# Values of mixer A and of mixer B's first group: from two transposed unit products to one product by tokens, with the rows carried to their blocks by transfers

## The chip, the cores and the metric

The kernel runs on one core of one Trainium2 chip. A core has TensorE (PE, the matrix products), VectorE (DVE), ScalarE (ACT), GpSimd (POOL) and SyncE (SP), which here only issues transfers, and 16 DMA engines that carry them out. Each engine takes its instructions strictly in the order in which the program has them. The metric is the device time of one execution in microseconds (us).

## The reference

One encoder layer over 512 tokens of 1024 channels, all in float32. What matters here is its first third: every mixer multiplies probabilities by values, and the values are columns of one product `h @ w_in`.

```
proj = h @ w_in[l]
qa, ka, va, qb, kb, vb = jnp.split(proj, SPLITS, axis=-1)
...
va = va.reshape(b, s, A_KV_HEADS, HEAD_DIM)
...
vb = vb.reshape(b, s, B_NG, B_HEADS_PER_GROUP, HEAD_DIM)
o_a = windowed_gqa_sink(qa, ka, va, a_sink[l])
o_b = dilated_mixture(qb, kb, vb)
```

Mixer A has 4 value heads of 64, 256 columns, and works in blocks of 128 tokens with a window of 128 to each side. Mixer B has 3 groups of 256 value columns, with windows and strides (128,1), (512,4) and (2048,16). Then come gates, an output product, a layer norm, a SwiGLU channel mixer of 2816 columns and a second layer norm. The change touches only how `va` and the first third of `vb` come about.

## The kernel before, in words

**Precision.** Every float32 operand is split into a high and a low part (h and l), and each product is three matmuls: high by high, high by low, low by high. So a weight tile of 128x512 is loaded into a staging slot, copied to its high part (ACT, or DVE where ACT is taken) and subtracted for its low part (DVE) before TensorE can use it.

**Order of the tokens.** The 512 tokens stand in x in four runs of 128: run r holds the tokens 4i+r. A block of 128 neighbouring tokens, which mixer A and B's first group need, therefore has 32 rows from each run.

**Products by features.** `feat_x` (line 466) makes 128 features of all 512 tokens: 8 steps of 3 matmuls of 512 columns (lines 456 to 458), with the weights as the stationary operand. Queries, keys and gates are made so. Values are wanted the other way round, with tokens on the partitions. Before the change `turned_values` (line 584) made two such units, evacuated each with its columns reordered into blocks, turned every block with two transposes on TensorE (line 611) and split the turned block into h and l with `value_split` (line 624). It ran once for mixer A ("VA") and, much later, once for B's first group ("V0"). The values of B's two dilated groups already came from `token_values` ("V"): x as the stationary operand and 512 value columns moving (lines 650 to 652), which gives 128 tokens by 512 columns at once; dilated groups can use a run of tokens as it is.

**Who sets the order.** The string `ORDER` (line 74) lists the steps: `q1` is a unit of queries, `k1` of keys, `T` turns up to four units by their rotary angles (for each unit two small SBUF-to-SBUF transfers there, line 485, and two back, line 506, with work on DVE between), `G` is a unit of gates, `A0` mixer A's heads 0 to 3 in four blocks, `B0` a head of mixer B. Each step hands its operations with a priority and a guessed cost to a list scheduler (`Program.run`), which writes one order for each engine at build time. Weights are asked for early (130 us of product time ahead, constant `LOOK`), as far as 6 staging slots and 16 slots for split weights allow. All loads and all small transfers go through the one queue of SP, and at most eight of its transfers are under way: each waits for the one eight places ahead of it.

**Inside a step of mixer A** (`unit_a`): scores on TensorE (lines 578, 579), scaling and maximum on DVE (line 726), exponential on ACT (line 730), reciprocal (733) and normalising on DVE or ACT (lines 666, 668), four transposes of probabilities (678), a copy (333) and a subtraction (683) to split them, and the product with the values (743, 744).

**The first group.** Before the second product of the program, three units are made together in eight steps as x arrives: the first of keys, the first of queries and the first of VA's two (`psk, psq, psv`, line 939).

Of the kernel before, what the change touches and what calls it, by code (L numbers as in the profile page):

```python
# [13 lines left out]
ALU = mybir.AluOpType  # L14
# [44 lines left out]
SPIN = 4  # L59

CUTS = ((0, 128), (128, 256), (256, 512))
FIRST = {("k", 0): (-1000, -998.2, -997.2), ("q", 0): (-998.8, -998.1, -997.1), ("v", 0): (-998.7, -998, -997),
         ("k", 1): (-996.9,), ("q", 1): (-996.7,), ("v", 1): (-996.6,),
         "x": (-999.9, -998.5, -997.5, -996.95, -996.8, -996.5, -996.4, -996.3)}
N_WS, N_WHL, N_ATT, N_WHL1, N_TWO = 6, 16, 16, 40, 4

# [31 lines left out]
class Program:  # L98
# [16 lines left out]
    def op(self, alts, fn, reads=(), writes=(), prio=0.0, after=(), abs_prio=None, moves=0.0):  # L115
        o = Op()
        o.urgent = self.urgent
        o.alts, o.fn = alts, fn
        o.prio = (self.T + prio if abs_prio is None else abs_prio, len(self.ops))
        o.ready, o.done, o.eng = 0.0, None, None  # L120
        deps = set(a for a in after if a is not None)
        for t in reads:
            deps.update(self.writer.get(t, ()))
        for t in writes:
            deps.update(self.writer.get(t, ()))
            deps.update(self.readers.get(t, ()))
# [162 lines left out]
def hybrid_layer(ctx: ExitStack, tc: tile.TileContext, wpack, xT, xtok, sink, bgate,  # L289
# [54 lines left out]
    def cp_alts(n, ps=False):  # L344
        return [(ACT, act(n, ps)), (DVE, dve(n, not ps))]
# [74 lines left out]

    first = {}
    for j in range(2):
        for w, u in (("k", U_KA), ("q", U_QA), ("v", U_VA)):
            first[w, j] = half_unit_by(u, j, ((0, S),) if j else CUTS, FIRST[w, j])
    for j in range(KD):
        st, ap = slot(F32, "xs"), FIRST["x"][j]
        load(st, xT[j], abs_prio=ap)
        th, tl = xtok_of(j)
        op(cp_alts(S), lambda e, j=j, st=st: copy(e, xh[j](), st.t), reads=[st], writes=[th], abs_prio=ap)
        op([(DVE, dve(S))], lambda e, j=j, st=st: nc.vector.tensor_tensor(  # L430
            xl[j](), st.t, f32(xh[j]()), op=ALU.subtract), reads=[st, th], writes=[tl], abs_prio=ap)
    cosT, sinT, mA, mB = slot(), slot(), slot(), slot()
# [32 lines left out]
    def feat_x(ps, wu):  # L465
        for k in range(KD):
            feat_k(ps, wu, k, XM, xtok_of)
# [113 lines left out]
        return go, [(qt, "h"), (qt, "l"), (kt, "h"), (kt, "d"), (kl, "h"), (kl, "d")]  # L581


    def turned_values(u, nt, turn_by=0, done=None):

        src = []
        w = S // nt
        for i in range(2):
            ps = done
            if i or not done:  # L590
                ps = bank("dense")
                feat_x(ps, unit(u + i))
            t = slot()

            def evac(e, t=t, ps=ps):
                s = view(ps.t, nt, True)
                if turn_by:
                    copy(e, view(t.t[:, turn_by * w:], nt - turn_by, False), s[:, :nt - turn_by])
                    copy(e, view(t.t[:, :turn_by * w], turn_by, False), s[:, nt - turn_by:])
                else:  # L600
                    copy(e, view(t.t, nt, False), s)

            op(cp_alts(S, True), evac, reads=[ps], writes=[t], prio=EV)
            src.append(t)
        res = []
        for b in range(NR):
            pb = bank("tb")

            def turn(e, pb=pb, b=b):
                for i in range(2):  # L610
                    nc.tensor.transpose(pb.t[:, i * P:(i + 1) * P], src[i].t[:, b * P:(b + 1) * P], ident.t)

            op([(PE, 0.22)], turn, reads=[*src, ident], writes=[pb])
            res.append(value_split(pb))
        return res

    def value_split(pb, c0=0):

        t = slot(F32R)
        v = lambda: t.t.rearrange("p (h c) -> p h c", h=4)  # L620
        s = lambda: pb.t[:, c0:c0 + 256].rearrange("p (h c) -> p h c", h=4)
        op(cp_alts(256, True), lambda e: copy(e, v()[:, :, 0:64], s()), reads=[pb],
           writes=[(t, "h"), (t, "room")], prio=EV)
        op([(DVE, dve(256))], lambda e: nc.vector.tensor_tensor(
            v()[:, :, 64:128], s(), f32(v()[:, :, 0:64]), op=ALU.subtract),
           reads=[pb, (t, "h")], writes=[(t, "l")], prio=EV)
        return t

    def vtok(t):
        return [(t, "h"), (t, "l")]  # L630

    def token_values():

        parts_ = []
        for k in range(KD):
            st, h, l = slot(F32, "ws"), slot(F32R, "whl"), slot(F32R, "whl")
            u, c = U_VB + k // 4, (k % 4) * 256
            load(st, wpack[u:u + 3:2, :, c:c + 256].rearrange("g p c -> p g c"),
                 dst=lambda st=st: st.t.rearrange("p (g c) -> p g c", g=2), prio=-LOOK)
            split(st, h, l, prio=-LOOK, hold=[(l, "room")])  # L640
            parts_.append((h, l))
        res = ([], [])
        for r in range(NR):
            ps = bank("dense")
            for k in range(KD):
                wh, wl = parts_[k]

                def go(e, ps=ps, k=k, wh=wh, wl=wl, r=r):
                    a, b = xh[k]()[:, r * P:(r + 1) * P], xl[k]()[:, r * P:(r + 1) * P]
                    mm(ps.t, a, wh.t, start=(k == 0), stop=False)  # L650
                    mm(ps.t, a, wl.t, start=False, stop=False)
                    mm(ps.t, b, wh.t, start=False, stop=(k == KD - 1))

                op([(PE, 3 * pe(S))], go, reads=[wh, wl, *xtok_of(k)], writes=[ps])
                pr.T += 3 * pe(S)
            for g in range(2):
                res[g].append(value_split(ps, 256 * g))
        return res


# [275 lines left out]
        feat_x(ps, unit(u))  # L936
        return env["turn"].add(ps, *post)

    psk, psq, psv = bank("dense"), bank("dense"), bank("dense")
    for k in range(KD):  # L940
        for w, ps in (("k", psk), ("q", psq), ("v", psv)):
            feat_k(ps, [first[w, 0], first[w, 1]], k, XM, xtok_of)
    env = {"gate": 0, "qs": {}, "ks": {}, "turn": Turn()}
    ka = env["turn"].add(psk, k_post, 4)
    qa = env["turn"].add(psq, q_post, 4, (0, 0))
    load(mB, maskb, prio=0)

    def step(w):
        if w == "T":
            env["turn"].turn()  # L950
            env["turn"] = Turn()
        elif w == "VA":
            env["va"] = turned_values(U_VA, 4, 0, psv)
        elif w[0] == "q":
            i = int(w[1])
            kv = (i // 2) % 2
            qa.extend(dense(U_QA + i, q_post, 4, (kv, kv)))
        elif w == "k1":
            ka.extend(dense(U_KA + 1, k_post, 4))
        elif w[0] == "A":  # L960
            g = int(w[1])
            for b in range(NR):
                unit_a(g, b, qa[4 * g:4 * g + 4], ka[g], env["va"])
        elif w[0] in "gG":
            for _ in range(int(w[1:] or 1)):
# [634 lines left out]
```

## Time and profile before

| what | value |
|---|---|
| median of 3 runs | 781.69 us (781.56 to 782.1) |
| the profiled execution | 781.53 us, of which its span, first to last instruction, is 779.8 us |
| granted TensorE clock | 0.998 |
| TensorE | 769.9 us busy, 4486 matmuls |
| VectorE | 652.5 us busy |
| ScalarE | 480.9 us busy |
| transfers issued by SP | 429 rows of its queue |

In the profile a group of instructions stands in one row: line, engine, operation, output and input tile, shape and count, then the busy time of the group in us and the mean of one in ns, then the idle time of the engine ahead of them with what ended it. Rows of the timeline give the start in us, the length, the engine and the operation; "x8" means eight in a row. SPq is the queue of transfers on SP: its length is the time that SP needs to issue one, and its landing comes later. A matmul's length overlaps with the next one's, so its pace is read from the distance of two starts.

### The profile page before, as it was taken

The numbers are of one execution on the slowest core, as the hardware profiler recorded it, in microseconds if no ns is written. First come the engines' busy times: TensorE is split into PE (matmuls) and PEld (weight loads), VectorE is DVE, ScalarE is ACT, GpSimd is POOL, SyncE is SP. The second block draws the span as 40 slices with busy tenths as digits, with TensorE's granted clock in tenths as the row PEclk, the third lists the DMA queues.
The fourth block names the chain that finished last, engine by engine and source line by source line (L and its number), as shares of the span: only waits on it lengthen the run. The fifth ranks groups of instructions, "written<-read, shape, count | busy, mean of one in ns | idle before, by whom it ended". The sixth has DMA issues, their size and how long they took to land.

```text
span 779.8 us, 13408 instructions
## 1 busy us (share of the span) xinstructions
PE 769.9 (99%) x4486; PEld 676.6 (87%) x4486; DVE 652.5 (84%) x1377; ACT 480.9 (62%) x1061; POOL 131.5 (17%) x304
## 2 busy tenths in 40 slices
PE   9999999999999999999999999999999999999996
PEld 5888888888888888888888899999999999999985
DVE  5689889898778999797687999887988889888697
ACT  5557787868757668794341667566655566555631
POOL 4100001100000801600011010242102331123002
PEclk9999999999999999999999999999999999999999
DMA  8642323213132324436373388689867987689102
GB/s 268 217 138 71 99 88 105 83 44 108 57 96 88 104 87 145 142 111 201 121 217 67 109 231 225 155 183 213 227 179 161 241 179 208 182 213 210 52 1 108
DMA packets 64901, 111.79 MB, mean 143 GB/s; under 512 B 8640, under 2 KB 12352, under 8 KB 64832
## 3 DMA queue, kind: packets, MB, share of 16 engines
q1 hardware_dynamic: 52656, 89.37, 35.5%
q0 software_dynamic: 12032, 21.50, 16.5%
q8 instruction: 35, 0.57, 0.3%
q14 instruction: 34, 0.28, 0.1%
q10 hardware_dynamic: 144, 0.07, 0.0%
HBM read 104.09 MB, written 3.93 MB: 139 GB/s over the span
## 4 chain that ended last, share of the span: by engine, by line
PE 93%; DVE 2%; ACT 1%; DMA 1%; issue 1%; SPq 1%; DVEq 0%
PE ps L457 11%; PE ps L456 11%; PE ps L458 11%; PE ps L1314 9%; PE ps L1313 9%; PE ps L1312 9%; PE ps L1441 4%; PE ps L1442 4%; PE ps L1443 4%; PE ps L1077 3%; PE ps L1079 3%; PE ps L1078 3%; PE ps L678 2%; PE ps L579 1%; PE ps L578 1%; PE ps L743 1%
## 5 line engine op out<-in xcount | busy, mean ns | idle before, releaser
L333 ACT ACTIVATE sl<-sl 128x512 fp32r<-128x512 f32 (+5 forms) x446 | 242.5, 571 | 65.9 <-DMA sl<-wpack 16.6
L1196 DVE TENSOR_TENSOR sl<-sl,sl 128x512 fp32r<-128x512 f32 (+3 forms) x304 | 169.9, 604 | 12.1 <-ACT sl L333 7.6
L333 ACT ACTIVATE sl<-ps 128x256 f32<-128x256 f32 (+4 forms) x206 | 88.6, 451 | 114.5 <-PE ps L1314 66.6
L456 PE MATMUL ps<-x,sl 128*128 128x512 f32 x336 | 133.7, 398 | 0.4 <-ACT sl L333 0.3
L457 PE MATMUL ps<-x,sl 128*128 128x512 f32 x336 | 131.9, 393 | 0.2 <-DVE x L430 0.2
L458 PE MATMUL ps<-x,sl 128*128 128x512 f32 x336 | 131.6, 392 | 0.0
L354 DVE TENSOR_TENSOR sl<-sl,sl 128x512 fp32r<-128x512 f32 x130 | 87.0, 687 | 9.3 <-ACT sl L333 6.5
L1266 POOL DMA_DIRECT2D sl<-wpack x44 | 39.8, 970 | 260.1 <-DMA sl<-wpack 111.6
L458 PEld LDWEIGHTS ps<-x,sl 128*128 128x128 f32 x336 | 63.1, 188 | 14.4 <-DVE sl L382 0.7
L1312 PE MATMUL ps<-x,sl 128*128 128x256 f32 x264 | 74.8, 283 | 0.0
L1314 PE MATMUL ps<-x,sl 128*128 128x256 f32 x264 | 74.7, 283 | 0.0
L1313 PE MATMUL ps<-x,sl 128*128 128x256 f32 x264 | 74.7, 283 | 0.0
L456 PEld LDWEIGHTS ps<-x,sl 128*128 128x128 f32 x336 | 63.2, 188 | 12.2 <-ACT x L333 1.0
L457 PEld LDWEIGHTS ps<-x,sl 128*128 128x128 f32 x336 | 63.3, 188 | 12.0 <-DVE x L430 1.8
L1196 DVE TENSOR_TENSOR sl<-sl,ps 128x512 f32<-128x512 f32 (+1 forms) x78 | 47.4, 611 | 25.7 <-PE ps L1314 16.6
L1312 PEld LDWEIGHTS ps<-x,sl 128*128 128x128 f32 x264 | 50.6, 192 | 0.5
L1313 PEld LDWEIGHTS ps<-x,sl 128*128 128x128 f32 x264 | 50.6, 192 | 0.5
L1314 PEld LDWEIGHTS ps<-x,sl 128*128 128x128 f32 x264 | 50.6, 192 | 0.0
L1314 PE MATMUL ps<-tw,sl 128*128 128x256 f32 x176 | 49.8, 283 | 0.0
L1313 PE MATMUL ps<-tw,sl 128*128 128x256 f32 x176 | 49.8, 283 | 0.0
L1314 PE MATMUL ps<-sl,sl 128*128 128x256 f32 x176 | 49.8, 283 | 0.0
L1313 PE MATMUL ps<-sl,sl 128*128 128x256 f32 x176 | 49.8, 283 | 0.0
(149 smaller groups left out, 1808.7 us busy)
## 6 DMA issues: line engine op xcount, KB each, us to landing
sl<-wpack SPq DMA_DIRECT2D x243, 256.0 KB, 3.4
sl<-wpack POOLq DMA_DIRECT2D x44, 256.0 KB, 5.2
wf<-wpack SPq DMA_DIRECT2D x36, 256.0 KB, 4.2
wf<-wpack POOLq DMA_DIRECT2D x36, 256.0 KB, 6.5
sl<-sl SPq DMA_DIRECT2D x88, 32.0 KB, 1.9
sl<-xT SPq DMA_DIRECT2D x8, 256.0 KB, 5.8
sl<-xtok SPq DMA_DIRECT2D x8, 256.0 KB, 2.7
gz<-sl SPq DMA_DIRECT2D x7, 256.0 KB, 2.2
```

The lines of the kernel that those rows point to most:

```text
L333: nc.scalar.activation(dst, src, AF.Copy)
L354: op([(DVE, dve(S))], lambda e: nc.vector.tensor_tensor(l.t, src.t, f32(h.t), op=ALU.subtract), reads=[src, h], writes=[l], prio=prio, abs ...
L456: mm(o, a, x0, start=(k == 0), stop=False)
L457: mm(o, a, x1, start=False, stop=False)
L458: mm(o, b, x0, start=False, stop=(k == nk - 1))
L1196: op([(DVE, dve(w))], lambda e: nc.vector.tensor_tensor(dst(), x(), y(), op=o), reads=reads, writes=writes, prio=prio)
L1266: return op([(POOL, 1.0)], lambda e: nc.gpsimd.dma_start(dst.t, wpack[u, :, j * S:(j + 1) * S], accum_op=ALU.add), reads=[dst], writes=[ds ...
L1312: mm(o, wh, bh[k](), start=(first and k == 0), stop=False, skip_group_check=True)
L1313: mm(o, wh, bl[k](), start=False, stop=False, skip_group_check=True)
L1314: mm(o, wl, bh[k](), start=False, stop=(k == 3), skip_group_check=True)
L1441: mm(ps.t, x0, w[0].t, start=(first and m == 0), stop=False, skip_group_check=True)
L1442: mm(ps.t, x0, w[1].t, start=False, stop=False, skip_group_check=True)
```

## The change

`token_values` gets an argument. With `dilated` true it does what it did. With false it makes the values of mixer A and of B's first group together: 256 columns of VA and 256 of V0 form 512 moving columns, and four products of 24 matmuls, one for each run of tokens, give them all. Each product is evacuated by one plain copy of 128x512, and a new function `move` carries its rows to their blocks: four transfers of 32 rows by 256 columns for mixer A and eight of 16 rows by 256 columns for B's first group, whose blocks are shifted by 64 tokens. When all four products have been carried, the four block tiles are split into h and l by the same `value_split`, which now reads SBUF instead of PSUM.

The weights of this product lie in units of 128 columns, so each of its eight staged tiles is loaded by two transfers of 128 KB with rows of 512 bytes. `turned_values`, its 16 transposes and the late step V0 are gone. In the first group VA's unit is replaced by the second unit of queries ("r"), and the first `T` now turns four units. One of the seven gate units that were stored to DRAM and fetched again during mixer A now comes at the end of `ORDER`, where it is kept. The very first piece of x is copied by DVE instead of ACT.

```
 ORDER = """
-VA q1 T G q2 A0 q3 q4 G k1 T G A1 q5 G q6 q7 T A2 G G A3 G
-Q00 K00 T V Q02 K02 T V0 Q01 K01 T B0 B1 g Q10 K10 T g Q12 K12 T Q11 K11 T B2 B3 g7
+q2 VA T G A0 q3 q4 G k1 T A1 q5 G q6 q7 T A2 G G A3 G Q00 K00 T V Q02 K02 T Q01 K01 T B0 B1 g Q10 K10 T g Q12 K12 T Q11 K11 T B2 B3 g8
 """
...
+    def move(src, c, r, dst, n, at):
+
+        for b in range(P // n):
+            m, a = at(b)
+            op([(SP, 0.1)], lambda e, d=dst[m], a=a + n * r, b=b: nc.sync.dma_start(
+                d.t[a:a + n, c:c + 256], src.t[n * b:n * b + n, c:c + 256]), reads=[src], writes=[(dst[m], c, a + n * r)],
+               prio=EV)
...
-    def token_values():
+    def token_values(dilated):
...
+                for n, u in enumerate((U_VA, U_V0)):
+                    op([(SP, 0.37)], lambda e, st=st, n=n, u=u, k=k: nc.sync.dma_start(
+                        st.t[:, 256 * n:256 * n + 256].rearrange("p (g c) -> p g c", g=2),
+                        wpack[u:u + 2, :, k * P:k * P + P].rearrange("g p c -> p g c")), writes=[(st, n)], prio=-LOOK)
...
+        raw = [slot() for _ in range(0 if dilated else NR)]
         for r in range(NR):
             ps = bank("dense")
...
+            else:
+                t = slot()
+                op(cp_alts(S, True), lambda e, t=t, ps=ps: copy(e, t.t, ps.t), reads=[ps], writes=[t], prio=EV)
+                move(t, 0, r, raw, 32, lambda b: (b, 0))
+
+                move(t, 256, r, raw, 16, lambda b: ((b + 1) % 8 // 2, 64 * ((b + 1) % 2)))
+        for t in raw:
             for g in range(2):
-                res[g].append(value_split(ps, 256 * g))
+                n = 16 if g else 32
+                res[g].append(value_split(t, 256 * g, [(t, 256 * g, a) for a in range(0, P, n)]))
...
     ka = env["turn"].add(psk, k_post, 4)
-    qa = env["turn"].add(psq, q_post, 4, (0, 0))
+    qa = env["turn"].add(psq, q_post, 4, (0, 0)) + env["turn"].add(psr, q_post, 4, (0, 0))
...
         elif w == "VA":
-            env["va"] = turned_values(U_VA, 4, 0, psv)
+            env["va"], env["v0"] = token_values(False)
...
-        elif w == "V0":
-            env["v0"] = turned_values(U_V0, 8, 1)
         elif w == "V":
-            env["v1"], env["v2"] = token_values()
+            env["v1"], env["v2"] = token_values(True)
```

Two places of the built programs show what this moves.

The queue of SP in the kernel before, from the first small transfer to the last of the first `T`. `sl<-sl` of 16x512 are the transfers of `T` (there at line 485, back at line 506), `sl<-wpack` are loads of weights, `gz<-sl` stores a gate:

```order
L485 DMA sl_318<-sl_307 16x512 x2
L341 DMA sl_327<-wpack 128x512
L485 DMA sl_318<-sl_325 16x512 x2
...
L485 DMA sl_318<-sl_445 16x512 x2
L341 DMA sl_456<-wpack 128x512
L341 DMA sl_476<-wpack 128x512
L931 DMA gz_500<-sl_493 128x512
L506 DMA sl_307<-sl_318 16x512 x2
L506 DMA sl_325<-sl_318 16x512 x2
L506 DMA sl_445<-sl_318 16x512 x2
```

The same queue in the changed kernel, from the carrying of the first product's rows on (line 602 is `move`, line 505 the way back of `T`):

```order
L602 DMA sl_434<-sl_428 32x256
L602 DMA sl_436<-sl_428 32x256
...
L602 DMA sl_434<-sl_428 16x256
L505 DMA sl_317<-sl_331 16x512 x2
...
L602 DMA sl_434<-sl_480 32x256
...
L602 DMA sl_434<-sl_533 32x256
...
L602 DMA sl_434<-sl_533 16x256
L340 DMA sl_569<-wpack 128x512
L340 DMA sl_588<-wpack 128x512
```

Where small transfers came in twos to sixes between loads, there are now 12 for the first product, 8 of `T`, 12 for the second and 12 for the third product without a load between them: 44 in a row. Then come five loads, five transfers of the fourth product, one load and the other seven.

The queue of ACT in the kernel before, at mixer A's first transposes. Line 666 is normalising, line 730 the exponential, line 333 the common copy:

```order
L730 ACTIVATE sl_599,st_643<-sl_599,st_643 128x385
L666 ACTIVATE sl_593<-sl_593,st_624 128x256
L333 ACTIVATE sl_702<-sl_511 128x512
L730 ACTIVATE sl_602,st_643<-sl_602,st_643 128x385
L333 ACTIVATE sl_721<-ps_707 128x512
```

The same place in the changed kernel (line 332 is the common copy, line 663 normalising, line 924 a gate's bias). The 128x4x64 copies are the h parts of the eight value tiles; `sl_434` is the block tile whose last 16 rows are the last transfer of all:

```order
L727 ACTIVATE sl_695,st_707<-sl_695,st_707 128x385
L332 ACTIVATE sl_781<-sl_434 128x4x64
L332 ACTIVATE sl_788<-sl_436 128x4x64
...
L332 ACTIVATE sl_811<-sl_392 64x512
L332 ACTIVATE sl_817<-sl_715 128x512
L924 ACTIVATE sl_825<-ps_605,bg 128x512
L332 ACTIVATE sl_831<-ps_658 128x512
L663 ACTIVATE sl_656<-sl_656,st_666 128x256
L332 ACTIVATE sl_847<-sl_727 128x512
L332 ACTIVATE sl_853<-ps_756 128x512
L663 ACTIVATE sl_670<-sl_670,st_666 128x256
```

Seven copies of value tiles have moved ahead of the normalising of `sl_656` and `sl_670`, two of the four tiles that mixer A's first group of four transposes reads.

More of the change, by code (lines that the diff above doesn't have):

```diff
@@ L61 @@
 CUTS = ((0, 128), (128, 256), (256, 512))
-FIRST = {("k", 0): (-1000, -998.2, -997.2), ("q", 0): (-998.8, -998.1, -997.1), ("v", 0): (-998.7, -998, -997),
-         ("k", 1): (-996.9,), ("q", 1): (-996.7,), ("v", 1): (-996.6,),
+FIRST = {("k", 0): (-1000, -998.2, -997.2), ("q", 0): (-998.8, -998.1, -997.1), ("r", 0): (-998.7, -998, -997),
+         ("k", 1): (-996.9,), ("q", 1): (-996.7,), ("r", 1): (-996.6,),
          "x": (-999.9, -998.5, -997.5, -996.95, -996.8, -996.5, -996.4, -996.3)}
@@ L422, in hybrid_layer @@
     for j in range(2):
-        for w, u in (("k", U_KA), ("q", U_QA), ("v", U_VA)):
+        for w, u in (("k", U_KA), ("q", U_QA), ("r", U_QA + 1)):
             first[w, j] = half_unit_by(u, j, ((0, S),) if j else CUTS, FIRST[w, j])
@@ L428, in hybrid_layer @@
         th, tl = xtok_of(j)
-        op(cp_alts(S), lambda e, j=j, st=st: copy(e, xh[j](), st.t), reads=[st], writes=[th], abs_prio=ap)
+        op(cp_alts(S)[1 if j == 0 else 0:], lambda e, j=j, st=st: copy(e, xh[j](), st.t), reads=[st], writes=[th], abs_prio=ap)
         op([(DVE, dve(S))], lambda e, j=j, st=st: nc.vector.tensor_tensor(
@@ L581, in scores, with value_split @@
         return go, [(qt, "h"), (qt, "l"), (kt, "h"), (kt, "d"), (kl, "h"), (kl, "d")]
[L584 to L617, printed above, removed]
+    def value_split(ps, c0, toks):
         t = slot(F32R)
         v = lambda: t.t.rearrange("p (h c) -> p h c", h=4)
-        s = lambda: pb.t[:, c0:c0 + 256].rearrange("p (h c) -> p h c", h=4)
-        op(cp_alts(256, True), lambda e: copy(e, v()[:, :, 0:64], s()), reads=[pb],
+        src = lambda: ps.t[:, c0:c0 + 256].rearrange("p (h c) -> p h c", h=4)
+        op(cp_alts(256, True), lambda e: copy(e, v()[:, :, 0:64], src()), reads=toks,
            writes=[(t, "h"), (t, "room")], prio=EV)
         op([(DVE, dve(256))], lambda e: nc.vector.tensor_tensor(
-            v()[:, :, 64:128], s(), f32(v()[:, :, 0:64]), op=ALU.subtract),
-           reads=[pb, (t, "h")], writes=[(t, "l")], prio=EV)
+            v()[:, :, 64:128], src(), f32(v()[:, :, 0:64]), op=ALU.subtract),
+           reads=[*toks, (t, "h")], writes=[(t, "l")], prio=EV)
         return t
@@ L636, in token_values @@
             st, h, l = slot(F32, "ws"), slot(F32R, "whl"), slot(F32R, "whl")
[L637 to L640, printed above, removed]
+            if dilated:
+                u, c = U_VB + k // 4, (k % 4) * 256
+                load(st, wpack[u:u + 3:2, :, c:c + 256].rearrange("g p c -> p g c"),
+                     dst=lambda st=st: st.t.rearrange("p (g c) -> p g c", g=2), prio=-LOOK)
+                toks = [st]
+            else:
[3 more added lines that the diff above has]
+                        wpack[u:u + 2, :, k * P:k * P + P].rearrange("g p c -> p g c")), writes=[(st, n)], prio=-LOOK)
+                toks = [(st, 0), (st, 1)]
+            op(cp_alts(S), lambda e, h=h, st=st: copy(e, h.t, st.t), reads=toks, writes=[h, (l, "room")], prio=-LOOK)
+            op([(DVE, dve(S))], lambda e, h=h, l=l, st=st: nc.vector.tensor_tensor(
+                l.t, st.t, f32(h.t), op=ALU.subtract), reads=[*toks, h], writes=[l], prio=-LOOK)
             parts_.append((h, l))
         res = ([], [])
+        raw = [slot() for _ in range(0 if dilated else NR)]
         for r in range(NR):
@@ L655, in token_values @@
                 pr.T += 3 * pe(S)
+            if dilated:
+                for g in range(2):
+                    res[g].append(value_split(ps, 256 * g, [ps]))
+            else:
+                t = slot()
[3 more added lines that the diff above has]
+        for t in raw:
             for g in range(2):
-                res[g].append(value_split(ps, 256 * g))
+                n = 16 if g else 32
+                res[g].append(value_split(t, 256 * g, [(t, 256 * g, a) for a in range(0, P, n)]))
         return res
@@ L937, in dense @@
         return env["turn"].add(ps, *post)
-    psk, psq, psv = bank("dense"), bank("dense"), bank("dense")
+    psk, psq, psr = bank("dense"), bank("dense"), bank("dense")
     for k in range(KD):
-        for w, ps in (("k", psk), ("q", psq), ("v", psv)):
+        for w, ps in (("k", psk), ("q", psq), ("r", psr)):
             feat_k(ps, [first[w, 0], first[w, 1]], k, XM, xtok_of)
```

## Prediction

> **What bounds the kernel now.** I read the page first, then who TensorE waits for, then the chain, then the queues of the first 100 us.
>
> ```profile
> PE 769.9 (99%) x4486; PEld 676.6 (87%) x4486; DVE 652.5 (84%) x1377; ACT 480.9 (62%) x1061; POOL 131.5 (17%) x304
> PE 93%; DVE 2%; ACT 1%; DMA 1%; issue 1%; SPq 1%; DVEq 0%
> PE ps L409 <- DVE eps L443: 1.2, 1, 1.2
> PE ps L456 <- ACT sl L333: 0.3, 1, 0.3
> PE ps L457 <- DVE x L430: 0.2, 1, 0.2
> ```
>
> The first row says that TensorE is busy 99% of the span, the second that 93% of the chain that ended last is TensorE's own work, and the last three that it waits for others 1.7 us in all, at the start. So the time is the number of matmuls at their pace, plus what is spilled at the start and the end. Two rules follow for this change. A matmul that is removed gives back its pace in full. And a wait that is put in front of TensorE anywhere is lost in full, because there is no idle time behind it in which it could be made up.
>
> **The change part by part.**
>
> *Matmuls.* The two unit products of VA and the two of V0 were 4 x 24 matmuls of 512 columns; the new product is 4 runs x 24 of 512 columns. That is even. The 16 transposes go.
>
> ```profile
> 30.59 0.44 PE ps L611 x4
> L611 PE MATMUL ps<-ident,sl 128*128 128x128 f32 x16 | 2.4, 272 | 0.0
> ```
>
> In the chain four of them take 0.44 us, 0.11 each (the 272 ns of the group overlap). 16 x 0.11 = 1.8 us less on TensorE.
>
> *The weights of the new product.* They come in 16 transfers of 128 KB instead of 8 of 256 KB. The second product of the program (then VA's second unit, now the queries q2) starts at 23.63 and ends, 24 matmuls on, at 29.07:
>
> ```profile
> 23.63 0.39 PE L456 MATMUL ps<-x,sl 128*128 128x512 f32 x1
> 29.07 0.39 PE L456 MATMUL ps<-x,sl 128*128 128x512 f32 x1
> 2.60 1.38 SPq L378 DMA_DIRECT2D sl<-wpack  x3
> 16.10 5.53 SPq L341 DMA_DIRECT2D sl<-wpack  x10
> sl<-wpack SPq DMA_DIRECT2D x3, 128.0 KB, 4.9
> L354 DVE TENSOR_TENSOR sl<-sl,sl 128x512 fp32r<-128x512 f32 x130 | 87.0, 687 | 9.3 <-ACT sl L333 6.5 <-issue 0.9 <-ACT sl L927 0.5
> L333 ACT ACTIVATE sl<-sl 128x512 fp32r<-128x512 f32 x289 | 173.9, 624 | 52.0 <-DMA sl<-wpack 14.7 <-PE ps L457 14.5 <-DVE sl L1196 8.3
> ```
>
> The pace is 5.44 / 24 = 0.227 us a matmul. SP begins the loads after the first group at 16.1; two are q2's, so VA's begin near 17.2. Three loads in a row take 1.38 us, with the gap 0.475 each; 16 of them put the last at 17.2 + 15 x 0.475 = 24.3. It lands 4.9 later (the row of 128 KB), at 29.2, and is split by a copy (0.62) and a subtraction (0.69), at 30.5. TensorE wants it, the eighth of eight steps of 0.68, at 29.07 + 7 x 0.68 = 33.8. That edit costs nothing; its cover is 3.3 us.
>
> *The 48 carrying transfers.* This is the term that decides. The trace has no transfer of 32 or 16 rows by 256 columns, but it has the same kind from the same queue, 16 rows by 512 columns from SBUF to SBUF:
>
> ```profile
> 42.24 3.68 SPq L506 DMA_DIRECT2D sl<-sl  x6
> 86.49 4.95 SPq L506 DMA_DIRECT2D sl<-sl  x8
> 91.54 0.53 SPq L931 DMA_DIRECT2D gz<-sl  x1
> 125.53 4.36 SPq L506 DMA_DIRECT2D sl<-sl  x6
> 129.99 0.53 SPq L931 DMA_DIRECT2D gz<-sl  x1
> sl<-sl SPq DMA_DIRECT2D x88, 32.0 KB, 1.9
> sl<-wpack SPq DMA_DIRECT2D x243, 256.0 KB, 3.4
> ```
>
> Eight of them fill the queue from 86.49 to 91.54: 0.63 us each, though one moves 32 KB and a load moves 256 KB in 0.475. Landing takes 1.9, and eight may be under way, so landing would allow one every 0.24: it is the issuing that sets the pace. The bounds for a new one are a load's 0.475 below and 0.74 above (the train at 125.53, six in 4.46, with one slow one in it). I take 0.63: two thirds of the new ones have the same 16 rows, all have the same two sides, and bytes are evidently not what costs.
>
> The Trainium skill, "DMA: Bandwidth & Descriptors", section "Issuing engines are not separate DMA queues", holds that the time a sequencer needs to start a DMA is usually small beside the DMA itself. By that rule the queue would keep up and the time would be rival A's; the rows above, 0.63 for the issue against 0.24 for an eighth of a landing, do not bear it out here. The same page, section "Bandwidth", speaks against the change: transfers under 64 KB are dominated by their descriptors, with 0.68 us for 4 KB. At 0.68 for each of the 48 the sum below would be 2.4 us longer, an estimate from that page.
>
> *When they are done.* The new product's first run ends with a matmul that starts at 29.07 + 23 x 0.227 = 34.3 and takes 0.4; its evacuation takes 0.59 (below), so the carrying starts at 35.3. From there SP issues 44 small transfers without a break (12 for the first run, 8 of `T`, 12, 12): 44 x 0.63 = 27.7, to 63.0. Five loads, 2.4, to 65.4; five transfers, 3.1, to 68.5; one load, 0.5, to 69.0; the last of the other seven starts 6 x 0.63 later, at 72.8, and lands at 74.7.
>
> *Who waits for it.* ACT copies the eight value tiles in its fixed order. The first of seven 128x4x64 copies in a row reads the 16 rows that land last. Behind it stand, in this order, the six other copies, one of 64x512, one of 128x512, a gate, an evacuation, normalising 128x256, a copy of 128x512, an evacuation and again normalising 128x256. The two normalised tiles are the first and the fourth that mixer A's first transposes read.
>
> ```profile
> L333 ACT ACTIVATE sl<-sl 128x256 fp32r<-128x256 f32 x66 | 25.6, 409 | 4.9 <-DVE sl L1196 3.4 <-PE ps L1443 0.9 <-PE ps L1442 0.5
> L333 ACT ACTIVATE sl<-sl 64x512 fp32r<-64x512 f32 x43 | 26.9, 630 | 5.0 <-DMA sl<-sl 2.7 <-DVE sl L544 1.1
> L927 ACT ACTIVATE sl<-ps,bg 128x512 f32<-128x512 f32 x16 | 10.8, 683 | 9.1 <-DVE sl L500 4.5 <-PE ps L458 4.5
> L333 ACT ACTIVATE sl<-ps 128x512 f32<-128x512 f32 x13 | 7.7, 588 | 2.5 <-PE ps L458 2.4
> L666 ACT ACTIVATE sl<-sl,st 128x256 f32<-128x256 f32 x31 | 14.0, 500 | 1.0 <-DVE st L733 0.9
> 26.27 2.27 ACT L333 ACTIVATE sl<-sl 128x512 fp32r<-128x512 f32 x4
> ```
>
> Busy time by count: 7 x 0.39 + 0.63 + 2 x 0.60 + 0.68 + 2 x 0.59 + 2 x 0.45 = 7.3. Packed they go a little faster (four copies in 2.27 are 0.57 each, not 0.60), so 7.0: the fourth tile is ready at 81.7. DVE's seven subtractions run beside this and end earlier.
>
> *When TensorE wants it.* From 23.63 to the fourth transpose TensorE has q2 (24 matmuls), the new product (96), a gate (24), q3 (24), q4 (24) and 9 of the next gate: 201 x 0.227 = 45.6. Between them stand eight score matmuls of 256 columns and eight of 384, and three transposes.
>
> ```profile
> 60.55 0.87 PE ps L678 x8
> 248.82 0.47 PE ps L803 x4
> ```
>
> Four of 256 columns take 0.47, so eight take 0.9; eight of 384 columns are put at 0.17 each by the columns, 1.4 (an estimate from 0.227 for 512); three transposes at 0.11, 0.3. In all 48.2, so it arrives at 71.8.
>
> *The sum.* TensorE stands from 71.8 to 81.7: 9.9 us lost. In this stretch some 60 small transfers pass, and one train of the three quoted had one that took 0.7 more; I add one such, 0.7. From the median: 781.7 - 1.8 + 9.9 + 0.7 = 790.5. The profiled execution is 781.53 and its span 779.8; the 1.7 around it stay, and it is 0.2 under the median, so its like should be 790.3.
>
> *The small rest.* The late V0 leaves mixer B's stretch, which frees about as much of DVE and ACT there as it takes earlier: the evacuations and value splits keep their number and size. One gate less is stored and fetched, off the chain. The first piece of x is copied by DVE, but the matmul behind it waits for the low part, which needs DVE too, as before. I put these at nothing, within 1 us either way.
>
> **The rivals.**
>
> *A, the queue keeps up (faster).* The small transfers cost so little that ACT finds its rows landed. The wait is gone when the last one lands 9.9 us earlier; over 48 transfers that is a price of 0.63 - 0.21 = 0.42 or less. For it: they carry 16 or 32 KB where the quoted ones carry 32, and a load takes 0.43 without its gap. Against: eight times the bytes go for less, so halving them should not help. Time: 781.7 - 1.8 = 779.9.
>
> *B, they cost what loads cost (no change).* At 0.475 the train is 48 x 0.155 = 7.4 shorter, 2.5 of the wait are left: 781.7 - 1.8 + 2.5 = 782.4. For it: loads from the same queue. Against: every train of SBUF-to-SBUF transfers in the trace.
>
> *C, the new product starves as well (slower still).* Landings of rows of 512 bytes that take twice 4.9 us would use up the cover of 3.3 and start the carrying 1.6 to 2 us late: about 792.5. Against: the three landings of 128 KB above were taken in the busiest stretch.
>
> **How the numbers follow.** The wait at 0.475 to 0.74 a transfer gives 782 to 796; with 0.55 to 0.73, which I hold likely, 786.5 to 795. Chances: the forecast 0.77, A 0.08, B 0.09, C 0.06. The range runs from 783.5, where B ends, to 795.5; C lies in it. It leaves out A, B and a little above. A measurement of this kernel can tell about 0.2%, 1.6 us. Faster is A, 0.08; the same is B, 0.09; slower is the forecast and C, 0.83.
>
> **What would show it.** In the profile after: TensorE waiting some 10 us at its first probability transposes, once, near 72 us, released by ACT's normalising; ACT idle ahead of a copy that a small transfer releases; trains of line 602 at 0.63 each; 16 matmuls fewer. I am wrong if those trains run at 0.47 or less, or if TensorE stands elsewhere.

## The result, and the profile after

The changed kernel takes 792.55 us (median of 4 runs, 792.37 to 793.48) beside 781.78 for the kernel before on the same chip: ratio 1.0140, 95% interval 1.0122 to 1.0157. It is slower by about 11 us, 2 more than forecast.

The page of the changed kernel: its span, TensorE's busy time, the granted clock in 40 slices, and the shares of the chain.

```profile
span 790.7 us, 13461 instructions
PE 769.9 (97%) x4470; PEld 677.1 (86%) x4470; DVE 651.8 (82%) x1372; ACT 482.2 (61%) x1064; POOL 134.4 (17%) x304
PEclk9999899999999999999999999999999999999998
PE 90%; SPq 3%; DMA 2%; ACT 2%; DVE 1%; issue 1%; DVEq 0%; ACTq 0%
```

TensorE has 16 matmuls fewer and is busy just as long as before, so those that are left cost more somewhere; the 8 in the clock's fifth slice, 79 to 99 us, says where. Who TensorE waits for (us in all, times, the longest):

```profile
PE ps L675 <- ACT sl L663: 10.8, 3, 9.7
```

Two of these three times, 10.2 us together, are at mixer A's first probability transposes, for ACT's normalising; the third, 0.57, is at 344 us, in another stage. SP's queue, in order of time (start, us):

```profile
17.41 9.14 SPq L619 DMA_DIRECT2D sl<-wpack  x16
35.27 7.46 SPq L602 DMA_DIRECT2D sl<-sl  x12
...
48.20 15.91 SPq L602 DMA_DIRECT2D sl<-sl  x24
64.21 2.44 SPq L340 DMA_DIRECT2D sl<-wpack  x5
66.75 3.05 SPq L602 DMA_DIRECT2D sl<-sl  x5
70.49 4.63 SPq L602 DMA_DIRECT2D sl<-sl  x7
75.16 2.95 SPq L340 DMA_DIRECT2D sl<-wpack  x6
```

The queue is full from 35.3 to 78. A move costs 7.46 / 12 = 0.62 to 15.91 / 24 = 0.66. Behind 44 small transfers (36 moves and 8 of `T`) come five loads of weights, then the rest of the moves with one load among them, then six more loads. ACT in the same stretch, the bracket being the idle time ahead of a row and what ended it:

```profile
66.95 0.63 ACT L332 ACTIVATE sl<-sl 128x512 fp32r<-128x512 f32 x1 [9.12 <-DMA sl<-wpack]
...
69.60 2.79 ACT L332 ACTIVATE sl<-sl 128x512 fp32r<-128x512 f32 x5 [0.85 <-DMA sl<-wpack]
...
76.42 3.56 ACT L332 ACTIVATE sl<-sl 128x256 fp32r<-128x256 f32 x9 [1.28 <-DMA sl<-sl]
...
80.93 0.50 ACT L663 ACTIVATE sl<-sl,st 128x256 f32<-128x256 f32 x1
...
82.33 0.51 ACT L663 ACTIVATE sl<-sl,st 128x256 f32<-128x256 f32 x1
```

ACT stood 9.12 us at the first of the five loads, worked for the next 8 us but for 0.85 at another of these loads, and stood only 1.28 us more at the carried rows. Both tiles that TensorE wants come 4 to 6 us behind that. TensorE around the wait:

```profile
71.41 0.39 PE L457 MATMUL ps<-x,sl 128*128 128x512 f32 x1
81.49 0.90 PE L675 MATMUL ps<-ident,sl 128*128 128x128 f32 x3 [9.69 <-ACT sl L663]
82.89 1.33 PE L675 MATMUL ps<-ident,sl 128*128 128x128 f32 x5 [0.50 <-ACT sl L663]
...
85.30 0.63 PE L455 MATMUL ps<-x,sl 128*128 128x512 f32 x1
85.73 0.63 PE L456 MATMUL ps<-x,sl 128*128 128x512 f32 x1
...
86.75 0.39 PE L456 MATMUL ps<-x,sl 128*128 128x512 f32 x1
86.98 0.39 PE L457 MATMUL ps<-x,sl 128*128 128x512 f32 x1
```

It stands from 71.6 to 81.5. Then, until 86.5, its matmuls come 0.43 apart and not 0.23: half pace. The two stretches of this (length, busy time and count by engine, granted clock, DMA share, GB/s):

```profile
72.00:84.00 12.00, 2.01 (x9) 1.58 (x9) 9.71 (x26) 10.67 (x30) 1.72 (x4) 0.67 0.54 178
84.00:100.00 16.00, 16.00 (x79) 13.53 (x78) 12.30 (x33) 11.79 (x29) 2.12 (x8) 0.92 0.32 99
```

The sum: 16 transposes less, -1.8; 10.2 of standing at the transposes; about 0.9 of small waits elsewhere, the 0.57 at 344 us and the rest at the program's start; about 1.7 of half pace (TensorE is busy 769.9 here and 768.2 in e1_b_by_pool below, which has the same matmuls and no such wait). That is +11.0, and the spans differ by 790.7 - 779.8 = 10.9.

### The profile page after: what moved, and what is told of

It is laid out like the page before. It is cut to its first block, busy times and chain, and to the rows that moved or that the text cites. A ratio compares the mean times of both kernels' runs of the same rounds, so it can differ in the third digit from the quotient of the medians.

```text
span 790.7 us, 13461 instructions
## 1 busy us (share of the span) xinstructions
PE 769.9 (97%) x4470; PEld 677.1 (86%) x4470; DVE 651.8 (82%) x1372; ACT 482.2 (61%) x1064; POOL 134.4 (17%) x304
## 4 chain that ended last, share of the span: by engine, by line
PE 90%; SPq 3%; DMA 2%; ACT 2%; DVE 1%; issue 1%; DVEq 0%; ACTq 0%
PE ps L456 10%; PE ps L455 10%; PE ps L457 10%; PE ps L1309 9%; PE ps L1308 9%; PE ps L1307 9%; PE ps L1436 4%; PE ps L1437 4%; PE ps L1438 4%; SPq L602 3%; PE ps L1074 3%; PE ps L1073 3%; PE ps L1072 3%; PE ps L675 3%; PE ps L578 1%; PE ps L577 1%
## 5 line engine op out<-in xcount | busy, mean ns | idle before, releaser
L332 ACT ACTIVATE sl<-sl 128x512 fp32r<-128x512 f32 (+4 forms) x456 | 246.1, 568 | 80.0 <-DMA sl<-wpack 24.2
L1191 DVE TENSOR_TENSOR sl<-sl,sl 128x512 fp32r<-128x512 f32 (+3 forms) x304 | 169.9, 603 | 10.9 <-ACT sl L332 7.6
L332 ACT ACTIVATE sl<-ps 128x256 f32<-128x256 f32 (+4 forms) x195 | 85.4, 454 | 114.5 <-PE ps L1309 65.3
L455 PE MATMUL ps<-x,sl 128*128 128x512 f32 x304 | 121.4, 399 | 0.0
L456 PE MATMUL ps<-x,sl 128*128 128x512 f32 x304 | 119.9, 394 | 0.9 <-DVE x L429 0.9
L457 PE MATMUL ps<-x,sl 128*128 128x512 f32 x304 | 119.2, 392 | 0.0
L353 DVE TENSOR_TENSOR sl<-sl,sl 128x512 fp32r<-128x512 f32 x114 | 75.9, 686 | 16.4 <-ACT sl L332 15.6
L1309 PE MATMUL ps<-x,sl 128*128 128x256 f32 x264 | 74.7, 283 | 0.0
L1308 PE MATMUL ps<-x,sl 128*128 128x256 f32 x264 | 74.7, 283 | 0.0
L457 PEld LDWEIGHTS ps<-x,sl 128*128 128x128 f32 x304 | 57.4, 189 | 12.6
L456 PEld LDWEIGHTS ps<-x,sl 128*128 128x128 f32 x304 | 57.5, 189 | 11.7 <-DVE x L429 2.3
L455 PEld LDWEIGHTS ps<-x,sl 128*128 128x128 f32 x304 | 57.7, 190 | 10.9 <-ACT sl L332 0.7
L1308 PEld LDWEIGHTS ps<-x,sl 128*128 128x128 f32 x264 | 50.6, 192 | 0.5
L1307 PEld LDWEIGHTS ps<-x,sl 128*128 128x128 f32 x264 | 50.6, 192 | 0.5
L1309 PEld LDWEIGHTS ps<-x,sl 128*128 128x128 f32 x264 | 50.6, 192 | 0.0
L1308 PE MATMUL ps<-tw,sl 128*128 128x256 f32 x176 | 49.8, 283 | 0.0
L1309 PE MATMUL ps<-tw,sl 128*128 128x256 f32 x176 | 49.8, 283 | 0.0
L1309 PE MATMUL ps<-sl,sl 128*128 128x256 f32 x176 | 49.8, 283 | 0.0
L1307 PE MATMUL ps<-tw,sl 128*128 128x256 f32 x176 | 49.8, 283 | 0.0
```

The source lines that it names most:

```text
L332: nc.scalar.activation(dst, src, AF.Copy)
L353: op([(DVE, dve(S))], lambda e: nc.vector.tensor_tensor(l.t, src.t, f32(h.t), op=ALU.subtract), reads=[src, h], writes=[l], prio=prio, abs ...
L455: mm(o, a, x0, start=(k == 0), stop=False)
L456: mm(o, a, x1, start=False, stop=False)
L457: mm(o, b, x0, start=False, stop=(k == nk - 1))
L1191: op([(DVE, dve(w))], lambda e: nc.vector.tensor_tensor(dst(), x(), y(), op=o), reads=reads, writes=writes, prio=prio)
```

## The experiments

The theory at the start: each small move has a price at SP's issue, and all that is queued behind them is late. The kernel before took 781.78, 781.27, 781.14 and 781.19 in the four sessions, so small differences are taken between ratios; 0.001 is 0.78 us.

| kernel | median us | ratio to before, 95% |
|---|---|---|
| the change | 792.55 | 1.0140 (1.0122 to 1.0157) |
| e1_b_by_pool | 780.45 | 0.9990 (0.9981 to 0.9999) |
| e2_no_wait_b | 791.43 | 1.0131 (1.0116 to 1.0146) |
| e3_more_moves | 802.21 | 1.0267 (1.0252 to 1.0282) |
| e4_keep_warm | 790.75 | 1.0119 (1.0103 to 1.0136) |
| e6_loads_by_pool | 792.76 | 1.0148 (1.0134 to 1.0162) |
| e7_both | 790.54 | 1.0121 (1.0107 to 1.0135) |
| e10_loads_in_time | 790.38 | 1.0116 (1.0103 to 1.0129) |
| e11_in_time_no_wait | 785.83 | 1.0063 (1.0050 to 1.0076) |
| e5_dram | 791.28 | 1.0126 (1.0112 to 1.0140) |
| e9_true_price | 791.92 | 1.0134 (1.0120 to 1.0148) |
| e12_planned_pool | 786.37 | 1.0061 (1.0046 to 1.0077) |

**Two thirds of the moves from another queue.**

```diff
-            op([(SP, 0.1)], lambda e, d=dst[m], a=a + n * r, b=b: nc.sync.dma_start(
+            op([(SP, 0.1)], lambda e, d=dst[m], a=a + n * r, b=b: (nc.gpsimd if c else nc.sync).dma_start(
```

> The 32 moves of 16 rows (mixer B's columns) are issued from POOL's queue instead of SP's; every engine keeps its planned order of everything else. Theory (the issue train on SP is the cost): SP keeps 16 moves, 16 x 0.63 = 10 us instead of 30, so the five loads at the head of ACT's and DVE's queues come some 15 us earlier and mixer A's first probability transposes no longer wait: 779.9 to 781 us, one wait of ten us gone. It needs POOL to issue a move in 0.73 us or less (8 per run of 5.9 us); at 1.0 us POOL's last one lands near 69 and about 4 us of the wait stay, 785. Rival (the transfers themselves, their rows of 1 KB and their landing, are slow whoever issues them): no change, 792.5 us.

Measured 780.45. POOL's queue and SP's, start and us:

```profile
52.21 3.81 POOL L602 DMA_DIRECT2D sl<-sl  x8 [1.63 <-ACT sl L332]
```

```profile
45.40 5.46 SPq L602 DMA_DIRECT2D sl<-sl  x8
50.95 3.67 SPq L340 DMA_DIRECT2D sl<-wpack  x5
54.72 2.42 SPq L602 DMA_DIRECT2D sl<-sl  x4
```

The loads are issued from 51 instead of 64, all moves by 57 instead of 75, and TensorE has no wait there. The bytes and the landing (1.8 us in both kernels) are the same, so the rival falls: it is the issuing. POOL issues one in 0.48. This version is also just faster than the kernel before, by 0.8 us where 1.8 of transposes are gone. TensorE's busy time fell by 1.7; its waits are 2.7 us in place of 1.7, among them:

```profile
PE ps L456 <- DVE x L429: 0.6, 2, 0.4
PE ps L675 <- ACT sl L663: 0.6, 1, 0.6
```

The row of L675 is at 331 us, in another stage; the rest is at the program's start, as in the kernel before. Why they are longer is open.

**More moves, same bytes.**

```diff
-            op([(SP, 0.1)], lambda e, d=dst[m], a=a + n * r, b=b: nc.sync.dma_start(
-                d.t[a:a + n, c:c + 256], src.t[n * b:n * b + n, c:c + 256]), reads=[src], writes=[(dst[m], c, a + n * r)],
+            op([(SP, 0.1)], lambda e, d=dst[m], a=a + n * r, b=b: [nc.sync.dma_start(
+                d.t[a + i:a + i + 16, c:c + 256], src.t[n * b + i:n * b + i + 16, c:c + 256]) for i in range(0, n, 16)],
+               reads=[src], writes=[(dst[m], c, a + n * r)],
```

> Each of the 16 moves of 32 rows is issued as two of 16 rows: 16 transfers more, the same bytes, nothing else moved. Theory (price per transfer issued on SP): 16 x 0.63 = 10 us more of wait at the same place, 802.5 us, and the trains stay at 0.63 each. Rival (bytes or landing set the pace): no change, 792.5 us.

Measured 802.21, +9.9 in ratio for 16 transfers. SP's queue:

```profile
50.66 20.50 SPq L602 DMA_DIRECT2D sl<-sl  x32
```

20.50 / 32 = 0.64: a price by transfer, not by bytes. The time came out as forecast, but not by ten us more of wait at the same place. TensorE's waits:

```profile
PE ps L675 <- ACT sl L663: 11.5, 3, 10.4
PE ps L455 <- DVE st L723: 5.4, 1, 5.4
```

The wait at the transposes is only 0.7 longer, because TensorE now also stands 5.4 us ahead of it, for DVE's scaling, which stands behind the split of the same late load (DVE waits 14.78 us there, ACT 15.28), and its half-pace matmuls cost 3.8 more (busy 773.7 beside 769.9). The end of the wait at the transposes did move by about what the price says, from 81.49 to 90.68.

**TensorE kept busy through the wait.**

```diff
+        fill = 0 if warmed else 40
+        warmed.append(1)
...
+            for _ in range(fill):
+                mm(pb.t, warm[:, :P], warm, start=True, stop=True)
```

> Forty matmuls of 512 columns on a constant tile, whose result nobody reads, stand on TensorE just ahead of the first probability transposes: 40 x 0.227 = 9.1 us, inside the wait of 9.9. Nothing else is moved. Theory (after standing idle TensorE runs at about half pace for some 4 to 5 us, which costs 1.7 to 2 us beside the wait itself): the wait ends at the same time, and the half pace behind it goes: 790.8 us, matmuls 0.227 apart straight after the transposes. Rival (the half pace behind the wait comes from what is read or written there, not from standing idle): matmuls still 0.43 apart, 792.5 us or somewhat more.

Measured 790.75, -1.6 in ratio; spans 790.7 and 789.0. TensorE:

```profile
73.04 8.79 PE L680 MATMUL ps<-warm 128*128 128x512 bf16 x39 [1.49 <-DVE st L730]
81.67 1.19 PE L682 MATMUL ps<-ident,sl 128*128 128x128 f32 x8
...
82.93 0.40 PE L456 MATMUL ps<-x,sl 128*128 128x512 f32 x1
83.16 0.39 PE L457 MATMUL ps<-x,sl 128*128 128x512 f32 x1
```

The transposes start when they did (81.67 beside 81.49), and the matmuls behind them are 0.23 apart at once. So the half pace came from standing idle. (The 1.49 us of standing ahead of the fill did not bring it about: 39 fill matmuls in 8.79 are 0.225 apart.)

**What is late behind the train.** The prediction named the carried rows. This kernel takes away ACT's and DVE's wait for B's part of them, by reading A's columns in their place:

```diff
-                res[g].append(value_split(t, 256 * g, [(t, 256 * g, a) for a in range(0, P, n)]))
+                res[g].append(value_split(t, 0, [(t, 256 * g, a) for a in range(0, P, n)]))
```

> The four value copies and subtractions of mixer B's first group read mixer A's columns of the carried tile, so B's values are A's and nobody waits for the 32 moves of 16 rows, which are still issued in the same places. Theory (everything queued behind the train on SP is late, the loads too): ACT stood only 1.28 us at the carried rows after it had worked off loads that came 9.12 us late, so only 1.3 to 1.5 us go: 791.1 us. Rival (what counts is the last carried rows that the value copies read, as the prediction told it): the wait of 10.8 us goes wholly, 781 us.

Measured 791.43, -0.7 in ratio (less than the intervals can tell by themselves), spans -1.0. ACT:

```profile
66.82 0.63 ACT L332 ACTIVATE sl<-sl 128x512 fp32r<-128x512 f32 x1 [9.03 <-DMA sl<-wpack]
...
74.38 2.89 ACT L332 ACTIVATE sl<-sl 128x256 fp32r<-128x256 f32 x8
```

The rows are no longer waited for, but the load is, as before. TensorE's wait ends 1.8 us earlier (79.65 beside 81.49); but the half pace behind it lasts 6.4 us here and not 5.0, which takes back part of it. So the converse: the six loads from POOL's queue.

```diff
+            loads[0] += 1
+            (nc.gpsimd if loads[0] in AHEAD else nc.sync).dma_start(dst() if dst else b.t, src)
...
+AHEAD = range(22, 28)
```

> The six loads of weights that stand behind the carrying train on SP (five behind the third run's moves, one inside the fourth's) are issued from POOL's queue; all 48 moves stay on SP, and every engine keeps its planned order. Theory (two things are late behind the train, the loads at the head of ACT's queue and the carried rows in the middle of it, and either alone holds TensorE): ACT's 9.12 us wait for a load goes, but the train only gets shorter by 6 x 0.49 = 2.9 us, so its last rows land 2.9 us earlier and the wait ends 2.9 us earlier: 789.6 us. Rival (the late loads alone are the cost): 781 us.

> The six loads from POOL's queue as in e6_loads_by_pool, and mixer B's value copies read mixer A's columns as in e2_no_wait_b (B's first values are A's; all 48 moves are still issued). Theory: with both latenesses gone nothing at mixer A's transposes waits but the last four moves of 32 rows, which land near 67.5 with TensorE there at 71.5; the wait falls to at most 1.5 us: 780 to 781.5 us, though the two edits alone take 2.9 and 1.1 us. Rival (the two add up): 792.5 - 1.1 - 2.9 = 788.5 us.

Measured 792.76 and 790.54: neither forecast nor rival of either. In these kernels the lines from 340 on are 6 or 7 higher. POOL's queue and ACT in the second (the profiled execution took 792.53):

```profile
14.26 0.57 POOL L346 DMA_DIRECT2D sl<-wpack  x1 [4.36 <-DVE sl L388]
...
69.88 0.42 ACT L334 ACTIVATE sl<-sl 128x256 fp32r<-128x256 f32 x1 [6.03 <-DMA sl<-sl]
...
78.49 0.63 ACT L334 ACTIVATE sl<-sl 128x512 fp32r<-128x512 f32 x1 [2.69 <-DMA sl<-wpack]
```

Two things went wrong. POOL had nothing to do and issued the loads as soon as their buffers were free, from 14 us on, beside the program's first loads; the first move then started at 38.07 in e6 and 38.57 in e7, not at 35.27. And there is a third latecomer: with the first load early and B's rows not waited for, ACT stands 2.69 at the load that follows the train. So the loads once more, in time, with the six behind the train:

```diff
+AHEAD = range(22, 34)
...
+            ... b=b: (nc.gpsimd if (r, c, b) == (2, 256, 7) else nc.sync).dma_start(
```

> e6_loads_by_pool took the loads too early (from 14 us on, beside the first loads of the program, and TensorE came 2.8 us later). Here the same six loads, and the next six behind the train, are issued from POOL's queue behind one move (the last of the third run, which waits for that run's evacuation), so from 47 us on; the other 47 moves stay on SP, every engine's planned order is kept. Theory (loads and carried rows are late each for itself): the wait for loads goes, the last rows land some 3.5 us earlier, near 72.7, and ACT needs 5.0 to 6.4 us from them to the normalised tiles as before: 788 to 789.5 us. Rival (loads alone): 781 us.

> e10_loads_in_time with B's value copies reading A's columns (B's first values are A's; all 48 moves are still issued). In e7_both three things were late behind the train, the third being the load behind it (2.69 us of ACT's wait); here none of the three is, only the first move of the fourth run (lands near 65.4) is waited for. Theory (one train, several latecomers, of which the last one counts): the fourth tile is ready near 74.6 instead of 82.8 and TensorE waits about 3 us in all: 782.5 to 784.5 us, far more than the two edits alone give together. Rival (the edits add up): 792.5 - 1.1 - 3.5 = 788 us.

Measured 790.38 and 785.83. In ratio the rows alone give 0.7 us, the loads alone 1.9, both together 6.0: far more than the sum of 2.6, as the theory has it, though each number misses its forecast by about 1 us. The single gains are small beside the intervals; the end of TensorE's wait at the transposes says the same: 1.8 us earlier with the rows alone, 2.3 with the loads alone (79.24), 7.3 with both (74.24). ACT in the first and in the second of the two:

```profile
67.20 0.42 ACT L334 ACTIVATE sl<-sl 128x256 fp32r<-128x256 f32 x1 [5.65 <-issue]
...
74.17 3.56 ACT L334 ACTIVATE sl<-sl 128x256 fp32r<-128x256 f32 x9 [3.84 <-DMA sl<-sl]
```

```profile
66.14 0.42 ACT L334 ACTIVATE sl<-sl 128x256 fp32r<-128x256 f32 x1 [4.65 <-issue]
...
69.18 3.55 ACT L334 ACTIVATE sl<-sl 128x256 fp32r<-128x256 f32 x9
```

("issue" means that the profile shows no releaser.) With the loads in time ACT stands at the carried rows instead, twice, 9.5 us in all; the last land near 74.1, only 2.3 earlier, because 35 moves in a row now take 24.59, 0.70 each. Without B's rows as well it goes through at 69.18. What is left there is the first move of the fourth run, which is itself behind 35 others; the standing at the transposes falls from 10.2 to 3.4.

**Three other ways to carry.** Through DRAM, with 16 transfers:

```diff
+                op([(SP, 0.73)], lambda e, t=t, r=r: nc.sync.dma_start(
+                    vd.t[:, r, :], t.t), reads=[t], writes=[(vd, r)], prio=EV)
...
+                    raw[m].t[:, 0:256],
+                    vd.t[32 * m:32 * m + 32, :, 0:256].rearrange("i r c -> r i c")),
...
+                        raw[m].t[64 * h:64 * h + 64, 256:512],
+                        vd.t[16 * b:16 * b + 16, :, 256:512].rearrange("i r c -> r i c")),
```

> The carrying goes through DRAM: each run's tile is stored whole (4 stores of 256 KB), and the eight half tiles are fetched in 4 loads of 128 rows and 8 of 64, 16 transfers in place of 48; nothing is left out, and the planner orders ACT and SP anew around them. Theory (price per transfer issued): 32 transfers x 0.63 = 20 us less in SP's queue, the last fetch is issued near 62 us and lands near 65, before TensorE wants it: 780 to 781.5 us. Rival (a round trip through DRAM is longer than two moves inside SBUF, and the fourth run's fetches cannot start before its store has landed): the wait stays in part, 784 to 790 us.

Measured 791.28: the rival's mechanism, and more than its price. SP's queue and then ACT:

```profile
54.08 0.33 SPq L649 DMA_DIRECT2D vd<-sl  x1
...
58.30 2.39 SPq L654 DMA_DIRECT2D sl<-vd  x4
60.73 6.21 SPq L661 DMA_DIRECT2D sl<-vd  x8
```

```profile
61.68 0.42 ACT L332 ACTIVATE sl<-sl 128x256 fp32r<-128x256 f32 x1 [4.19 <-DMA sl<-vd]
...
67.88 0.42 ACT L332 ACTIVATE sl<-sl 128x256 fp32r<-128x256 f32 x1 [4.79 <-DMA sl<-vd]
```

The first fetch goes 4.2 us behind the last store, with two loads between, and a fetch of 64 rows costs 6.21 / 8 = 0.78 to issue. ACT's order, made anew, puts a copy of A's and one of B's values ahead of exponentials, and ACT stands 9.0 us at these two. The queue was free by 67, and still TensorE stood 7.6 us at the normalising.

The planner with the measured price:

```diff
-                        dma[0] = max(dma[0], now) + 0.45
+                        dma[0] = max(dma[0], now) + (0.63 if cost == 0.1 else 0.45)
```

> Only the planner's price of issuing one of the 48 moves is changed, from 0.45 to the measured 0.63 us; the same transfers from the same queue. It now lets the sixth load pass ahead of the fourth run's moves and puts three of the four normalised tiles ahead of mixer B's value copies on ACT. Theory (what hurts is not the train itself but that ACT's and DVE's fixed orders count on rows that come ten us later than planned): the first moves of the fourth run are issued by 66.5 and land by 68.5, the normalising follows at once, TensorE is there near 69.5: 780 to 782 us. Rival (the train is too long for any order, mixer A's values come too late as well): TensorE waits a little later for mixer A's values, 784 to 788 us.

Measured 791.92; neither the forecast nor the rival's place. TensorE's wait is still at the normalising, 5.9. ACT:

```profile
66.92 1.29 ACT L332 ACTIVATE sl<-sl 128x512 fp32r<-128x512 f32 x2 [2.00 <-DMA sl<-wpack]
...
71.39 0.63 ACT L332 ACTIVATE sl<-sl 128x512 fp32r<-128x512 f32 x1 [1.42 <-DMA sl<-wpack]
...
74.89 1.31 ACT L663 ACTIVATE sl<-sl,st 128x256 f32<-128x256 f32 x3 [0.98 <-DVE st L730]
```

The normalising does stand ahead of B's copies now. But the six loads are still issued behind 36 moves, from 64.04 on, and ACT is at them, some standing between, from 66.92 to 73.9. A truer price moved the rows and left the train.

Last, the planner is told that POOL carries B:

```diff
+            by = c > 0
+            op([(POOL, 0.48)] if by else [(SP, 0.1)], ...
+               prio=EV, moves=0.1 if by else 0.0)
```

> As e1_b_by_pool, mixer B's 32 moves from POOL's queue, but the planner knows of it: they are POOL's operations at 0.48 us each (the measured 3.81 for eight), so it orders ACT, DVE, POOL and TensorE anew. The only wait that e1_b_by_pool kept there was 0.6 us at the normalising. Theory (with the train cut to 16 moves the order no longer matters much): 779.9 to 781.5 us, TensorE at the first probability transposes some 5 us earlier and waiting less than 2 us. Rival (the earlier order finds ACT behind, as in e5_dram and e9_true_price): 783 to 786 us.

Measured 786.37, 783.1 to 787.7 over six runs: the rival, 0.4 above its range. The profiled one took 787.38. Same queues as in e1_b_by_pool, another order; ACT:

```profile
61.44 0.94 ACT L332 ACTIVATE sl<-sl 128x256 fp32r<-128x256 f32 x2 [4.49 <-DMA sl<-sl]
```

The planner's new order draws the transposes forward (TensorE is there at 67.3, not 71.6) and puts carried rows ahead of the exponentials, where ACT stands 4.49. Why the planner counts on these rows so early was not followed further.

## Why the prediction was right, and where not

- *TensorE bounds the kernel, so a wait is lost in full*: right. 10.2 of standing, 0.9 of small waits and 1.7 of half pace, less 1.8 of transposes, are the difference of the spans within 0.1.
- *16 transposes, -1.8*: right on TensorE (busy time -1.7 in e1_b_by_pool), where the gain shows; the time itself fell by 0.8.
- *The new weights cost nothing*: right. The 16 loads took 9.14, not 7.6, and the carrying still began at 35.27 (forecast 35.3).
- *0.63 a move at the issue*: right, 0.62 to 0.66; e3_more_moves and e1_b_by_pool show it by adding transfers and by taking them off. The rule of the Trainium skill, "DMA: Bandwidth & Descriptors", section "Issuing engines are not separate DMA queues", that starting from several engines saves only a time that is usually small, does not hold for such a train: a start takes 0.62 to 0.66 beside a landing of 1.8 to 1.9, but the landings overlap and the starts do not, and 32 starts moved to POOL are worth 11.7 us here (0.0150 in ratio).
- *The train ends at 63.0, the last move starts at 72.8 and lands at 74.7*: 1.1, 1.7 and 1.7 too early. The train of 24 ran at 0.66: one of its transfers took 1.41, the one dear transfer that the forecast had added as 0.7.
- *ACT needs 7.0 from there*: 6.4 (76.42 to 82.84). *TensorE is there at 71.8*: 71.6.
- *Lost 9.9, and 0.7 for one dear transfer*: 10.2 measured, so this term was 0.4 long.
- *The small rest, nothing within 1 us either way*: 0.9 of small waits, of which 0.57 at 344 us; e1_b_by_pool has them too.
- *What no step of the prediction had*: the half pace behind the wait, 1.7. With the small waits, and less the 0.4, that is the 2 us by which the sum fell short.
- *Who is waited for*: half right, and this is the step that failed. The prediction had the five loads in SP's order, but let ACT stand free until the last carried rows landed. ACT was held 9.12 us at the first of those loads, and the rows added 1.28. The named wait is real and ends last; with the loads in time and the rows still late the kernel is 9.1 us slower than before (e10_loads_in_time). But taking it away alone gains 0.7 us (e2_no_wait_b), because the loads hold ACT nearly as long. That the time came out nearly right although the prediction missed this is partly luck: both latecomers follow from one train, and they end 1.28 us apart.
- *Rival A* asked for 0.42 a move on SP and did not happen; its state was reached by the other queue. *B* (0.475) fell by the trains, *C* by the start at 35.27.

## What to carry to other kernels

Count the transfers on a queue before their bytes: a train of small ones delays everything queued behind it, and the engine that waits may stand at an unrelated load. When one cause makes several things late, undoing them one at a time shows almost nothing (0.7 and 1.9 us here, 6.0 together); shorten the queue instead, and see that what is moved to an idle queue does not run too early. A planner told a better price is not yet a better plan: on the same two queues the order that was planned with the wrong price (780.45) beat the one planned anew (786.37).

## What the runs showed that had not been expected

After standing idle TensorE runs at half pace for 5.0 us (6.4 in e2_no_wait_b): 9.85 us of standing cost about 1.7 more, and 40 matmuls whose result nobody reads took that away. The Trainium skill, "TensorE: Matmul & The Clock Gate", section "What's actually happening", describes this, with a window of about 3.4 us of idling ahead of it. In e11_in_time_no_wait a shorter stand was enough:

```profile
71.17 0.39 PE L464 MATMUL ps<-x,sl 128*128 128x512 f32 x1
74.24 0.73 PE L682 MATMUL ps<-ident,sl 128*128 128x128 f32 x3 [2.68 <-ACT sl L670]
...
77.55 0.63 PE L464 MATMUL ps<-x,sl 128*128 128x512 f32 x1
```

2.7 us of waiting, 3.1 between the starts, and the matmuls behind are at half pace, which 1.49 us of waiting in e4_keep_warm did not bring about. And POOL issues a small move in 0.48 where SP takes 0.62 to 0.70, though a load of 256 KB takes it longer (six in 3.41, 0.57 each, in e10_loads_in_time, beside 0.49).
